# Second expert's routing list moved ahead of the first expert's products, with its 0/1 matrices on VectorE and Silu's table loaded earlier

## The chip, the cores and the metric

The kernel runs on one core of one Trainium2 chip. The metric is the device time of one execution in microseconds; of several executions the median is taken. The core has TensorE (PE, with its weight loads PEld), VectorE (DVE), ScalarE (ACT), GpSimd (POOL) and SyncE (SP), which work through a queue of instructions each, in order, and wait for one another by semaphores. SyncE and GpSimd issue the DMAs.

## What is computed

One layer of a hybrid encoder over 512 tokens of width 1024: a Mamba-2 mixer and a forget-gate attention side by side, an output projection, a LayerNorm, then a mixture of experts with a second LayerNorm. The change is in the mixture, of which the reference is:

```python
g_logits = (hf @ rg_w + rg_b)                       # 4 groups
g_val, g_idx = lax.top_k(jax.nn.softmax(g_logits), 1)
e_logits = ...                                      # the 4 experts of the chosen group
e_val, e_idx = lax.top_k(jax.nn.softmax(e_logits), TOP_K)   # 2 of them
weights = g_val[:, None] * e_val / sum(e_val)
for e in range(N_EXPERTS):                          # 16
    act = jax.nn.silu(hf @ w_gate[e]) * (hf @ w_up[e])
    out = out + combine[:, e:e + 1] * (act @ w_down[e])
```

Each expert has w_gate and w_up of 1024x512 and w_down of 512x1024, in float32.

## The kernel before

**Stages.** Projections, scan and attention come first; in the last part of the attention the output projection (L807) and the LayerNorm of four blocks of 128 tokens (hh[0] to hh[3]) run. From each block the router's logits are computed, `choose` ranks them and `seat` numbers the tokens of each expert in `place` (token rows by expert). Then 16 experts are worked through, e = 0 to 15, called the first, second, third expert and so on here.

**An expert.** At most 128 tokens are taken for it. Its list comes in four steps. `seats_of` (L937) compares the seat numbers 1 to 128 with `place`, one 128x128 compare for each of the four token blocks, and so makes four 0/1 matrices `se` in bf16. `list_of` multiplies them by `entry` on TensorE (L945) into a PSUM bank `plist`; `entry` holds the token number in two columns and the token's weight in three (each weight is split into three bf16 parts, L1324 and L1326). VectorE reduces the bank to the index `ix` (L950, L951) and the weight `wc` (L954). `gather` (L958) is an indirect DMA, issued by GpSimd, that fetches the 128 token rows from the stored `hb` into `xgs[e % 2]`. `call(e)` does these steps in turn; with `weights=False` only the token columns are multiplied, and the `se` are kept for the weights later.

**Products.** All products are in float32 by splitting: each operand has a high part, rounded by ScalarE (`eh` of the weights L987, `xgh` of the tokens L90), and a low part, the difference by VectorE (`el` L988, `xgl` L91); high x high, low x high and high x low are summed in PSUM. `gate_up(e)` (L1004 to L1006) goes through eight pieces of gate and up weights, in four steps of two pieces and 12 products; four buffers of `eh` and four of `el` go round. Then Silu on ScalarE (L1012) and the product with up on VectorE (`ac`, L1014 or L1016) follow. `xg_T` (L980) transposes the next expert's gathered rows on TensorE into `pxg`, `act_T` (L1022) transposes `ac` into `pat`, and `down` runs one expert later, inside the loop of the next. So between the first expert's last product and the second's first one there is no down product.

**The first expert** doesn't wait for all tokens. Its rows of the first two blocks are gathered ahead (`gather_first`), and those of the last two are picked from hh[2] and hh[3] with 0/1 matrices `pick` (L1296); both are summed on TensorE in the banks `px` (L1291), already transposed. Then `split` makes `xgh` and `xgl` of px.

**Weights.** `weigh()` is a generator: up to its `yield` it forms the exponentials (Exp on ScalarE, L1305 and L1314), after it the weights of both chosen experts (L1316 to L1326) into `entry`. The router calls its first half by `next(wg)`; the second half is emitted by `drop(wg)` after the first expert's early steps.

**What sets the order.** TensorE's order is that of the code (`MANUAL`). VectorE, ScalarE and GpSimd keep the code's order inside `with tc.manual_schedule(engines=VECTOR)` (the router, L1334 on); what comes after it, such as `call` in the expert loop and the second half of `weigh`, is placed by the scheduler, which may also put it among the router's own instructions. In the expert loop `gate_up(0)` is advanced by three steps (`EARLY`); the second expert's `call(1, False)` comes after the first of these steps, the third's `call(2, False)` after the third. `weights_of_first()`, in the second expert's turn, makes the first expert's list, then the weights of the second and third, then counts the tokens (`pcnt`, L1413). `bank("s", ...)` gives these lists two PSUM banks in turn.

Of the kernel before, what the change touches and what calls it, by code (L numbers as in the profile page):

```python
# [40 lines left out]
EARLY = 3  # L41
# [28 lines left out]
def hybrid_layer(ctx: ExitStack, tc: tile.TileContext, x, xT, wu, w16, bT, bz, bv, b16, cw, cb,  # L70
# [861 lines left out]
    def seats_of(pool, place_, eng):  # L932

        r = (Q("se") if pool is lp else pool.tile([P, 256], F32, name="se")).bitcast(BF16)
        r = [r[:, t * P:(t + 1) * P] for t in range(NT)]
        for t in range(NT):
            eng.tensor_scalar(r[t], seats, place_(t), None, op0=OP.is_equal)  # L937
        return r
# [26 lines left out]
    def entry_of(e):  # L965
        return lambda t: entry[:, t, EO[e]]

    def call(e, weights=True):
        se = seats_of(lp, lambda t: place[:, t, EO[e]:EO[e] + 1], G)
        ix, wc = list_of(lp, se, entry_of(e), weights=weights)  # L970
        gather(ix, xgs[e % 2])
        lists[e] = [ix, wc if weights else se]
# [325 lines left out]
    def weigh():  # L1298

        gs, r1, wv, mx, gx = R([], "gs"), R([], "r1"), R([2], "wv"), R([5], "mx"), R([4], "gx")  # L1300
        oh = [R([4, 4], "oh") for _ in range(2)]
        lr = rows_(lg4)
        V.tensor_reduce(rows_(mx), lr, axis=AX.X, op=OP.max)
        V.tensor_tensor(lr, lr, over(rows_(mx), 4), op=OP.subtract)
        A.activation(gx, lg4[:, :, 0], AF.Exp)  # L1305
        og = CH["og"][:, :, :, None].to_broadcast([P, NT, 4, 4])
        for k in (1, 0):
            V.scalar_tensor_tensor(oh[k], CH["rank"][:, :, 1:5], float(k), og, op0=OP.is_equal, op1=OP.mult)
            if k:
                t_ = R([4, 4], "t_")  # L1310
                V.tensor_tensor(t_, oh[k], lg4[:, :, 1:5], op=OP.mult)
                oh0, oh1 = (o_.rearrange("p t g e -> p t (g e)") for o_ in oh)
                V.tensor_reduce(r1, t_.rearrange("p t g e -> p t (g e)"), axis=AX.X, op=OP.add)
                A.activation(r1, r1, AF.Exp)  # L1314
        yield
        V.tensor_reduce(gs, gx, axis=AX.X, op=OP.add)  # L1316
        V.scalar_tensor_tensor(gs, r1, 1.0, gs, op0=OP.add, op1=OP.mult)
        V.reciprocal(wv[:, :, 0], gs)
        V.tensor_tensor(wv[:, :, 1], wv[:, :, 0], r1, op=OP.mult)
        for k, o_ in enumerate((oh0, oh1)):  # L1320
            V.scalar_tensor_tensor(o_, o_, 1.0 / ALPHA, over(wv[:, :, k], 16), op0=OP.mult, op1=OP.mult)
        V.tensor_tensor(oh0, oh0, oh1, op=OP.add)
        for j in range(2, 5):
            V.tensor_copy(entry[:, :, :, j], oh0)  # L1324
            if j < 4:
                V.tensor_tensor(oh0, oh0, entry[:, :, :, j], op=OP.subtract)  # L1326
# [7 lines left out]
    with tc.manual_schedule(engines=VECTOR):  # L1334
        for t in range(NT):
            ph_ = proj_half(t, 0)
            if t == 3:
                next(ph_)
                seat(0, 2)
                gf = gather_first()  # L1340
                next(gf)
                next(ph_)
                u_T(2, 0)
                u_T(2, 1)
                drop(gf)
                norm_gain(2)
            drop(ph_)
            if t in DSP0:
                dsp[0, DSP0.index(t)] = wsplit(raw[0, DSP0.index(t)])
            if t:  # L1350
                norm_shift(t - 1)
                if t < 3:
                    u_T(t - 1, 0)
                    u_T(t - 1, 1)
                    norm_gain(t - 1)
                norm_bias(t - 1)
            ph_ = proj_half(t, 1)
            if t < 3:
                if t == 2:
                    logits(1)  # L1360
                    norm_store(1, hb, G)
                    norm_store(1, ub, G)
                    choose(0, 2)
                drop(ph_)
                norm_stats(t)
                if t == 1:
                    logits(0)
                    norm_store(0, hb, G)
                    norm_store(0, ub, G)
        next(ph_)  # L1370
        next(ph_)
        u_T(3, 0)
        drop(ph_)
        logits(2, range(3))
        px_open()
        u_T(3, 1)
        logits(3, range(4))
        norm_stats(3)
        norm_store(2, hb, G)
        norm_shift(3)  # L1380
        norm_gain(3)
        logits(3, range(4, 8))
        px_open()
        logits(2, range(3, 8))
        choose(2, 4)
        px_add(xgs[0], identf, range(KC))
        seat(2, 4)
        for t in (2, 3):
            picks(t)
        norm_bias(3)  # L1390
        norm_store(3, hb, G)
        px_add(hh[2], pick[2], range(KC))
        dsp[0, 2] = wsplit(raw[0, 2])
        wg = weigh()
        next(wg)
        xt_ = [wide("x", n, NX).rearrange("p (k s) -> p k s", s=P) for n in ("xgh", "xgl")]
        for hf in range(2):
            px_add(hh[3], pick[3], range(4 * hf, 4 * hf + 4), True)
            split(*(t_[:, hf * 4:hf * 4 + 4] for t_ in xt_), px[hf].rearrange("p (k s) -> p k s", s=P))
        for t in range(2, 4):  # L1400
            norm_store(t, ub, G)
        load_pieces(NPRE, NPRE + GATED, G)
        dsp[0, 3] = wsplit(raw[0, 3])

    def weights_of_first():

        lists[0] = list_of(lp, seats_of(lp, lambda t: place[:, t, EO[0]:EO[0] + 1], G), entry_of(0))
        for e in (1, 2):
            lists[e][1] = list_of(lp, lists[e][1], entry_of(e), tokens=False)[1]

        pn = bank("s", "pcnt")[:, :16]
        for tt in range(NT):
            T.matmul(pn, lhsT=onesb, rhs=mskb[:, tt], start=(tt == 0), stop=(tt == NT - 1))  # L1413
        V.tensor_reduce(cnt_i, pn, axis=AX.X, op=OP.max)
        rt.close()

    at = {}
    for e in range(NEXP - 2):
        load_pieces(NPRE + 12 * e + (0 if e else GATED), NPRE + 12 + 12 * e)
        gu = gate_up(e, xt_, "pj" if e else "o")  # L1420
        for n in range(EARLY):
            next(gu)
            if e == 0 and n == 0:
                call(1, False)
        call(e + 2, bool(e))
        if e == 0:
            drop(wg)
        if e == 1:
            weights_of_first()
        drop(gu)  # L1430
        xt_ = xg_T(xgs[(e + 1) % 2])
        for d in DOWN[e]:
            def between(f):
                if f == ACT_AT and d != e and e in DOWN[e]:
                    at[e] = act_T(e)
            finish(d, down(d, at.pop(d), between=between))
        if e not in DOWN[e]:
            at[e] = act_T(e)
# [182 lines left out]
```

## Time and profile before

| what | us |
|---|---|
| median of 3 runs | 629.06 |
| lowest and highest of them | 626.08, 634.25 |
| the profiled execution | 632.85 |
| its span, first to last instruction | 631.1 |
| TensorE busy in the span | 578.6 (92%) |
| VectorE busy | 526.4 (83%) |
| ScalarE busy | 409.7 (65%) |
| GpSimd busy | 195.8 (31%) |

All durations are of the one profiled execution, in us from the span's start. Busy shares are means over stages with different limits: what a change is worth is read where it stands. A duration of a TensorE product includes its way through the array; the pitch from one start to the next is what it takes from the stream.

### The profile page before, as it was taken

What the parts mean: (1) busy time and instruction counts of PE and PEld (TensorE: products, weight loads), DVE (VectorE), ACT (ScalarE), POOL (GpSimd) and SP (SyncE); (2) the same over time, 40 slices, a digit from 0 to 9 for tenths busy, and PEclk for the clock granted to TensorE, in tenths of its full rate; (3) what the DMA queues carried; (4) which work ended last, traced back from release to release, by engine and by line L of the source; (5) the groups of instructions that cost most, each with busy time, mean ns of one, the idle gap of its engine ahead of it and who ended that gap; (6) DMA issues with size and microseconds to landing.
All of it is one profiled execution on the core that took longest, in us unless ns stands there. A gap on an engine that the chain in (4) does not pass through costs nothing.

```text
span 631.1 us, 9108 instructions
## 1 busy us (share of the span) xinstructions
PE 578.6 (92%) x3020; PEld 472.7 (75%) x3021; DVE 526.4 (83%) x904; ACT 409.7 (65%) x640; POOL 195.8 (31%) x221
## 2 busy tenths in 40 slices
PE   6997997899999989999789999999999999999790
PEld 4786887788777758778667888888888888877550
DVE  3897598888668787668778999999999999999883
ACT  5575363543577776422267888888888888888660
POOL 6300000033553441014472223433343233412341
PEclk9998898999999999999889999999999999999996
DMA  8621021221222174994799999999999999998531
GB/s 264 209 68 60 8 77 59 84 68 65 70 68 66 36 238 133 389 344 175 281 389 319 304 382 344 386 361 358 355 346 342 328 352 373 346 339 287 190 122 61
DMA packets 62102, 142.73 MB, mean 226 GB/s; under 512 B 10073, under 2 KB 10073, under 8 KB 62048
## 3 DMA queue, kind: packets, MB, share of 16 engines
q1 hardware_dynamic: 55712, 127.88, 56.4%
q0 software_dynamic: 6336, 14.20, 7.6%
q8 instruction: 25, 0.41, 0.3%
q14 instruction: 29, 0.24, 0.1%
HBM read 136.26 MB, written 14.68 MB: 239 GB/s over the span
## 4 chain that ended last, share of the span: by engine, by line
PE 52%; DVE 16%; DMA 16%; issue 7%; ACT 6%; POOL 2%; POOLq 0%; SPq 0%; ACTq 0%; DVEq 0%
DMA xg<-ub,ix 6%; PE pw L807 4%; PE pg L1004 4%; PE pg L1006 4%; PE pg L1005 4%; PE pjT L241 4%; PE pu L1004 4%; PE pu L1006 4%; PE pu L1005 4%; PE py L1043 3%; PE py L1041 3%; PE py L1042 3%; DMA ub<-yo,ix 3%; PE pjR L265 3%; DMA xg<-hb,ix 2%
## 5 line engine op out<-in xcount | busy, mean ns | idle before, releaser
L987 ACT ACTIVATE eh<-wf 128x1024 fp32r<-128x1024 f32 x188 | 198.7, 1060 | 49.6 <-PE pg L1006 16.4
L1004 PE MATMUL pg<-eh,xgh 128*128 128x512 f32 x128 | 53.3, 416 | 0.8 <-ACT xgh L90 0.8
L958 POOL DMA_INDIRECT xg<-hb,ix x16 | 21.5, 1343 | 99.9 <-PE pg L1006 77.6
L1006 PE MATMUL pg<-eh,xgl 128*128 128x512 f32 x128 | 50.2, 393 | 1.3 <-DVE xgl L91 1.3
L1049 POOL DMA_INDIRECT ub<-yo,ix x14 | 27.2, 1945 | 74.5 <-ACT at L90 57.7
L937 POOL TENSOR_SCALAR se<-seats,place 128x128 bf16<-128x128 f32 x64 | 49.5, 784 | 1.6 <-PE pat L1022 1.1
L1004 PE MATMUL pu<-eh,xgh 128*128 128x512 f32 x128 | 49.9, 390 | 0.0
L1006 PE MATMUL pu<-eh,xgl 128*128 128x512 f32 x128 | 49.8, 389 | 0.0
L1041 PE MATMUL py<-eh,at 128*128 128x512 f32 x120 | 48.5, 404 | 1.0 <-ACT at L90 0.7
L241 PE MATMUL pjT<-xh,wh 128*128 128x512 f32 x112 | 47.6, 425 | 1.6 <-DVE kl L671 1.6
L1043 PE MATMUL py<-eh,at 128*128 128x512 f32 x120 | 47.1, 392 | 0.0
L241 PE MATMUL pjT<-xh,wl 128*128 128x512 f32 x112 | 45.0, 402 | 0.0
L241 PE MATMUL pjT<-xl,wh 128*128 128x512 f32 x112 | 45.0, 402 | 0.0
L265 PE MATMUL pjR<-wh,xh 128*128 128x256 f32 x128 | 38.6, 302 | 1.2 <-DVE vf L643 1.2
L265 PE MATMUL pjR<-wl,xh 128*128 128x256 f32 x128 | 37.5, 293 | 0.0
L265 PE MATMUL pjR<-wh,xl 128*128 128x256 f32 x128 | 37.4, 292 | 0.0
L130 POOL TENSOR_TENSOR rst<-rst,mhalf 128x1 f32<-128x1 f32 x8 | 4.6, 578 | 100.5 <-DVE rst L129 100.5
L1006 PEld LDWEIGHTS pg<-eh,xgl 128*128 128x128 f32 x128 | 24.1, 188 | 7.4 <-DVE xgl L91 2.2
L225 POOL TENSOR_TENSOR wl<-wr,wh 128x512 fp32r<-128x512 f32 x16 | 21.4, 1362 | 25.9 <-ACT wh L220 25.9
L1004 PEld LDWEIGHTS pg<-eh,xgh 128*128 128x128 f32 x128 | 24.2, 189 | 5.3 <-ACT xgh L90 1.2
L220 ACT ACTIVATE wh<-wr 128x1024 fp32r<-128x1024 f32 x22 | 23.1, 1054 | 7.5 <-PE pjT L241 3.4
L1006 PEld LDWEIGHTS pu<-eh,xgl 128*128 128x128 f32 x128 | 24.0, 188 | 5.1
(971 smaller groups left out, 1756.4 us busy)
## 6 DMA issues: line engine op xcount, KB each, us to landing
wf<-in_w_up SPq DMA_DIRECT2D x64, 512.0 KB
wf<-in_w_gate SPq DMA_DIRECT2D x64, 512.0 KB
wf<-in_w_down SPq DMA_DIRECT2D x62, 512.0 KB
wr<-in_wu SPq DMA_DIRECT2D x22, 512.0 KB
wor<-in_w_out SPq DMA_DIRECT2D x8, 512.0 KB
hh<-in_x SPq DMA_DIRECT2D x4, 512.0 KB
hb<-hh POOLq DMA_DIRECT2D x4, 512.0 KB, 4.8
ub<-hh POOLq DMA_DIRECT2D x4, 512.0 KB, 5.6
```

The source lines that it names most:

```text
L220: A.activation(h_, wr_, AF.Copy)
L241: T.matmul(pt, lhsT=w_[:, k % 4, m * P:(m + 1) * P], rhs=x_[k], start=(i == 0), stop=(i == 23))
L265: T.matmul(pt, lhsT=x_[k][:, t * P:(t + 1) * P], rhs=w_[:, k % 4, :], start=(i == 0), stop=(i == 23))
L807: T.matmul(pw, lhsT=m_[k][:, ts_], rhs=wo[k][w_][:, c_], start=(i == 0), stop=(i == 11))
L937: eng.tensor_scalar(r[t], seats, place_(t), None, op0=OP.is_equal)
L987: A.activation(h_, src, AF.Copy)
L1004: T.matmul(pt, lhsT=h_[:, k], rhs=wh_[:, f], start=(k == 0), stop=False)
L1005: T.matmul(pt, lhsT=h_[:, k], rhs=wl_[:, f], start=False, stop=False)
L1006: T.matmul(pt, lhsT=l_[:, k], rhs=wh_[:, f], start=False, stop=(k == KC - 1))
L1041: T.matmul(pt, lhsT=h_[:, f], rhs=wh_[:, c_], start=(f == 0), stop=False)
L1043: T.matmul(pt, lhsT=l_[:, f], rhs=wh_[:, c_], start=False, stop=(f == 3 and rows is None))
L1049: G.indirect_dma_start(out=ub, out_offset=bass.IndirectOffsetOnAxis(ap=ix, axis=0), in_=yo, in_offset=None, bounds_check=S - 1, oob_is_err ...
```

## The change

- The second expert's 0/1 matrices are made by VectorE, in the router, right after the LayerNorm's last step (`se1`), and its list and gather are called in the router, before the first expert's products, instead of after the first of the early steps.
- The first expert's 0/1 matrices, for its weights, are made earlier, after the third expert's call; its list is multiplied after the weights of the second and third expert instead of before them.
- A Silu of a 128x4 tile that nobody reads follows the second Exp; the load of Silu's table comes there.

```diff
-    def call(e, weights=True):
-        se = seats_of(lp, lambda t: place[:, t, EO[e]:EO[e] + 1], G)
+    def call(e, weights=True, se=None):
+        se = se or seats_of(lp, lambda t: place[:, t, EO[e]:EO[e] + 1], G)
...
                 A.activation(r1, r1, AF.Exp)
+
+                A.activation(R([], "tab"), r1, AF.Silu)
         yield
...
         norm_store(3, hb, G)
+        se1 = seats_of(lp, lambda t: place[:, t, EO[1]:EO[1] + 1], V)
         px_add(hh[2], pick[2], range(KC))
...
             split(*(t_[:, hf * 4:hf * 4 + 4] for t_ in xt_), px[hf].rearrange("p (k s) -> p k s", s=P))
+        call(1, False, se1)
         for t in range(2, 4):
             norm_store(t, ub, G)
...
     def weights_of_first():
 
-        lists[0] = list_of(lp, seats_of(lp, lambda t: place[:, t, EO[0]:EO[0] + 1], G), entry_of(0))
         for e in (1, 2):
             lists[e][1] = list_of(lp, lists[e][1], entry_of(e), tokens=False)[1]
+        lists[0] = list_of(lp, lists[0], entry_of(0))
...
-        for n in range(EARLY):
+        for _ in range(EARLY):
             next(gu)
-            if e == 0 and n == 0:
-                call(1, False)
         call(e + 2, bool(e))
         if e == 0:
             drop(wg)
+            lists[0] = seats_of(lp, lambda t: place[:, t, EO[0]:EO[0] + 1], G)
```

What stands where, before (-) and now (+). First VectorE, between the LayerNorm's last step (L1182) and the router's weights (`arena` tiles hold their small operands):

```order
 L1182 SCALAR_TENSOR_TENSOR hh<-hh,rs_3307,l1b 128x1024
-L988 TENSOR_TENSOR el__3365<-wf,eh 128x1024
+L937 TENSOR_SCALAR se<-seats,place 128x128 x4
+L988 TENSOR_TENSOR el__3370<-wf,eh 128x1024
 L1303 TENSOR_REDUCE arena_3188<-lg_3028 128x20
```

Four compares are added ahead of a weight piece's low part. A little further on VectorE's queue comes to the low half of the first expert's tokens (L91, twice):

```order
+L1323 SCALAR_TENSOR_TENSOR arena_3373<-arena_3373,arena_3188 128x64
+L1324 TENSOR_TENSOR arena_3188<-arena_3188,arena_3373 128x64
+L1326 CAST entry<-arena_3188 128x64
+L1328 TENSOR_TENSOR arena_3188<-arena_3188,entry 128x64
+L1326 CAST entry<-arena_3188 128x64
+L1328 TENSOR_TENSOR arena_3188<-arena_3188,entry 128x64
+L1326 CAST entry<-arena_3188 128x64
 L91 TENSOR_TENSOR xgl<-px,xgh 128x512 x2
-L1321 SCALAR_TENSOR_TENSOR arena_3368<-arena_3368,arena_3188 128x64
-L988 TENSOR_TENSOR el__3398<-wf,eh 128x1024
-L1322 TENSOR_TENSOR arena_3188<-arena_3188,arena_3368 128x64
```

The seven operations that end the weights have moved from behind the low halves to in front of them. On ScalarE, at the same place, the high halves of the tokens (L90) follow the two Exp:

```order
 L1305 ACTIVATE arena_3188<-lg_3028 128x16
 L1314 ACTIVATE arena_3188<-arena_3188 128x4
+L1316 ACT_TABLE_LOAD
+L1316 ACTIVATE arena_3373<-arena_3188 128x4
 L90 ACTIVATE xgh<-px 128x512 x2
 L987 ACTIVATE eh<-wf 128x1024 x7
-L1012 ACT_TABLE_LOAD
```

The table's load has moved from the first Silu to in front of the high halves. On GpSimd, after the stores of the normalized blocks, xg_3013 is the buffer of the second expert's gather:

```order
 L1188 DMA hb<-hh 128x1024 x2
+L937 TENSOR_SCALAR se<-seats,place 128x128 x8
+L958 DMA xg_3013<-hb,ix 128x1024
 L1188 DMA ub<-hh 128x1024 x2
 L925 DMA wf<-in_w_down 128x1024 x2
-L937 TENSOR_SCALAR se<-seats,place 128x128 x8
-L958 DMA xg_3013<-hb,ix 128x1024
```

Eight compares stand in front of the gather as before, now those of the third and the first expert; four DMA issues have moved behind it. Last, VectorE at `weights_of_first`, as it stands now (the fourth expert's index and weight, the second's weight, a weight piece, the third's weight, the first's list, the count):

```order
L950 TENSOR_REDUCE if__3669<-plist 128x1
L954 TENSOR_REDUCE wc<-plist 128x1
L951 TENSOR_SCALAR ix<-if__3669 128x1
L954 TENSOR_REDUCE wc<-plist 128x1
L988 TENSOR_TENSOR el__3766<-wf,eh 128x1024
L954 TENSOR_REDUCE wc<-plist 128x1
L950 TENSOR_REDUCE if__3697<-plist 128x1
L954 TENSOR_REDUCE wc<-plist 128x1
L951 TENSOR_SCALAR ix<-if__3697 128x1
L1418 TENSOR_REDUCE cnt_i<-pcnt 128x1
```

Before, the first expert's three reductions stood ahead of the second's weight, and the weight piece between the second's and the third's:

```order
L950 TENSOR_REDUCE if__3682<-plist 128x1
L954 TENSOR_REDUCE wc<-plist 128x1
L951 TENSOR_SCALAR ix<-if__3682 128x1
L954 TENSOR_REDUCE wc<-plist 128x1
L988 TENSOR_TENSOR el__3765<-wf,eh 128x1024
L954 TENSOR_REDUCE wc<-plist 128x1
L1414 TENSOR_REDUCE cnt_i<-pcnt 128x1
```

The weight piece keeps its place behind the second expert's weight; what has moved is that the first expert's reductions come behind both.

## Rows read from the trace of the kernel before

**Rows 1.** Windows: busy us by engine, PEclk, DMA share, GB/s.
```profile
303.00:304.00 1.00, 0.71 (x3) 0.71 (x4) 0.31 (x2) 0.00 (x0) 0.00 (x0) 0.50 0.90 295
...
327.00:328.00 1.00, 0.89 (x4) 0.89 (x5) 0.00 (x0) 0.00 (x0) 1.00 (x3) 0.50 1.02 377
350.00:360.00 10.00, 10.00 (x49) 8.09 (x48) 10.00 (x13) 7.88 (x10) 1.85 (x1) 1.00 0.93 294
```

**Rows 2.** Timeline of TensorE: start, us, engine, line, operation, [idle before <- releaser].
```profile
303.29 3.50 PE L1291 MATMUL px<-identf,xg 128*128 128x128 f32 x16 [1.71 <-DMA xg<-hb,ix]
...
307.62 3.84 PE L1291 MATMUL px<-xg,hh 128*128 128x128 f32 x32 [0.67 <-DVE xg L1296]
...
313.11 0.50 PE L1006 MATMUL pg<-eh,xgl 128*128 128x512 f32 x1 [0.37 <-DVE xgl L91]
...
323.87 0.39 PE L1006 MATMUL pu<-eh,xgl 128*128 128x512 f32 x1
327.11 1.97 PE L980 MATMUL pxg<-identf,xg 128*128 128x128 f32 x8 [2.85 <-DMA xg<-hb,ix]
...
330.44 0.40 PE L1006 MATMUL pg<-eh,xgl 128*128 128x512 f32 x1
```

**Rows 3.** Timeline of GpSimd, 309 to 332 us.
```profile
309.32 0.53 POOL L1188 DMA_DIRECT2D hb<-hh  x1 [9.12 <-DVE hh L1182]
...
311.99 7.27 POOL L937 TENSOR_SCALAR se<-seats,place 128x128 bf16<-128x128 f32 x8
319.72 1.39 POOL L958 DMA_INDIRECT xg<-hb,ix  x1 [0.46 <-issue]
...
329.60 2.34 POOL L937 TENSOR_SCALAR se<-seats,place 128x128 bf16<-128x128 f32 x4 [1.09 <-PE pat L1022]
```

**Rows 4.** VectorE's groups by form, 290 to 343 us: busy, mean ns | idle before.
```profile
L1324 DVE CAST entry<-arena 128x64 bf16<-128x64 f32 x3 | 0.8, 263 | 0.0
...
L1273 DVE TENSOR_SCALAR se<-seats,place 128x128 bf16<-128x128 f32 x2 | 0.5, 282 | 0.0
...
L1326 DVE TENSOR_TENSOR arena<-arena,entry 128x64 f32<-128x64 f32 x2 | 0.4, 224 | 0.0
...
L1322 DVE TENSOR_TENSOR arena<-arena,arena 128x64 f32<-128x64 f32 x1 | 0.4, 385 | 0.0
...
L1321 DVE SCALAR_TENSOR_TENSOR arena<-arena,arena 128x64 f32<-128x64 f32 x1 | 0.2, 207 | 0.0
```

**Rows 5.** Timeline of VectorE, 312 to 327 us.
```profile
312.38 1.27 DVE L91 TENSOR_TENSOR xgl<-px,xgh 128x512 fp32r<-128x512 f32 x2
...
326.28 0.41 DVE L1016 TENSOR_TENSOR ac<-sg,pu 128x256 f32<-128x256 f32 x1
```

**Rows 6.** Timeline of ScalarE, 311 to 330 us.
```profile
311.27 0.21 ACT L1314 ACTIVATE arena<-arena 128x4 f32<-128x4 f32 x1 [0.43 <-DVE arena L1313]
311.38 1.07 ACT L90 ACTIVATE xgh<-px 128x512 fp32r<-128x512 f32 x2
...
322.44 1.28 ACT L1012 ACT_TABLE_LOAD   x1
323.74 0.38 ACT L1012 ACTIVATE sg<-pg 128x256 f32<-128x256 f32 x1
...
329.61 1.05 ACT L987 ACTIVATE eh<-wf 128x1024 fp32r<-128x1024 f32 x1
```

**Rows 7.** Timeline of TensorE and VectorE at the lists, 338 to 341 us.
```profile
338.10 1.23 DVE L988 TENSOR_TENSOR el__3755<-wf,eh 128x1024 fp32r<-128x1024 f32 x1
...
339.51 0.51 PE L945 MATMUL plist<-entry,se 128*128 128x3 bf16 x8 [0.99 <-DVE wc L954]
...
339.80 0.16 DVE L954 TENSOR_REDUCE wc<-plist 128x1 f32<-128x3 f32 x1
...
339.88 1.23 DVE L988 TENSOR_TENSOR el__3765<-wf,eh 128x1024 fp32r<-128x1024 f32 x1
...
340.02 0.24 PE L1413 MATMUL pcnt<-mskb,onesb 128*128 128x16 bf16 x4
```

## Prediction

> **What bounds the kernel now.** I read the windows first, then TensorE's timeline, then that of each engine it waits for. From 350 us on TensorE is busy in all of a 10 us window, at granted clock 1.00 [rows 1]; it goes on so, expert after expert, to the last ones. A delay or a gain before that point is therefore carried to the end one for one. So the question is when that dense stretch begins, and the change works just ahead of it, between 307 and 341 us. There the reader is to see three things. First, TensorE finishes gathering the first expert's tokens (the px products, 32 from 307.62 for 3.84, so until 311.46) and its first product with the low half of the tokens starts at 313.11 [rows 2]. Second, the last product of the first expert starts at 323.87 and, with the products at a pitch of about 0.23, ends near 324.1; then TensorE waits 2.85 for the second expert's gather, and the first transposes after it, 8 in 1.97, run at granted clock 0.50 [rows 1, 2]. Third, at 339.51 a 0.99 wait for VectorE stands inside the lists [rows 7].
>
> The gather that it waits for started at 319.72, behind eight 0/1 compares on GpSimd from 311.99 to 319.26, and behind four more DMA issues from 309.85 on, where the store of 309.32 ends [rows 3]. From its start to the transposes of 327.11 are 7.39.
>
> **The change part by part.** Times are those of the profiled execution (632.85 us, span 631.1), and the sum is a difference against it; it lies 3.8 above the median 629.06 of the runs, whose own spread is 626.08 to 634.25. I carry the difference over to the median.
>
> (1) The gather comes earlier, by less than the words of the change say. VectorE makes the second expert's compares, but the order shows that GpSimd still has eight in front of the gather, now those of the third and the first expert. Only the four DMA issues go behind it. So the compares start at 309.85 instead of 311.99 and, at the same 7.27, end at 317.1; with the 0.46 that lay between compares and gather the gather starts near 317.6, its list being ready at 316.7 (low halves of (2) from 315.0 for 1.27, two reductions of 0.15 and their handovers), and its rows are there 7.39 later, at 325.0. At the 0.59 a compare that four took from 329.60 [rows 3], instead of 0.91, the list would be what it waits for: 324.2. The stores and loads moved behind it are not needed before the second expert is through.
>
> (2) The first products start later, because of VectorE. Before, the low half (xgl, L91) starts at 312.38 [rows 5]. Now four compares stand ahead of it; two took 0.5, 0.282 each [rows 4], so four are 1.13 by durations, about 0.9 end to end. And the rest of the weights (seven small operations: one L1321 of 0.21, L1322 0.39, three L1324 of 0.263, two L1326 of 0.224, together 1.83 [rows 4]), which before ran after the low half, stand ahead of it as well, as the order shows. By durations 2.96; eleven short operations overlap by up to 0.07 each, 2.2 at least. I take 2.6: the low half starts at 315.0, the first product with it at 315.7 for 313.11.
>
> (3) ScalarE's table. The load took 1.28 at 322.44, and Silu's first use followed at 323.74 [rows 6]; there it delayed nobody, for TensorE waited for the gather until 327.11. It now stands between the Exp of 311.27 and the copies xgh of 311.38, which TensorE's first products read. Exp ends about 311.5 + 0.9 (the compares) = 312.4; load 1.28 and the small Silu 0.21 (as the Exp row) make 313.9, the first copy (half of 1.07) 314.4. So the high half comes 2.4 late, but the low half of (2) is later still, and the load costs nothing of its own; without (2) it would be the bound. The Trainium skill ("ScalarE: Activation LUTs", What ACT_TABLE_LOAD costs) counts a drain of about 1.38 us beside the load, about 2.66 in all. By that rule the high half would be there at 315.8, TensorE at 316.4 and the sum 0.7 larger; here Silu starts 1.30 after the load does, so the trace shows no such drain.
>
> (4) The clock. Between the px products with the new list (until about 311.6) and the first product at 314.4 TensorE has nothing to do for 2.8. After gaps of 1.71 and 2.85 the rows show clock 0.50, the 1.2 GHz level (windows 303 and 327); after 0.67 the products of 307.62 ran at 0.12 each, near the pace of 2.4 GHz [rows 1, 2]. 16 products took 3.50 at the low clock, 32 took 3.84 at the full one [rows 2], so such a stretch loses up to 3.50 - 1.92 = 1.6. A part of it falls on the wait for the low half; I take 1.0, bounds 0 and 1.6.
>
> (5) End of the first expert: 324.1 + 2.6 - 0.1 (a list moved out of it) + 1.0 = 327.6. The gather is there at 325.0, so that wait is gone, but the transposes start 0.5 later than at 327.11. What is late next is ScalarE and VectorE: the order puts the copy and the difference of the second expert's fourth weight piece in front of the tokens' split, and the copy waits for the last product to release its buffer. Copy 1.05 [rows 6], difference 1.23 [rows 7], product ac 0.41, low half 0.64 [rows 5], and four handovers: about 3.4 from the transposes' start to the first low product. Before, with the transposes at half clock, it was 330.44 - 327.11 = 3.33 [rows 2]. So the half clock that goes is replaced by a chain as long: +0.1, together +0.6.
>
> (6) In that chain TensorE works about 1.8 of 3.4, with two waits of roughly 1 us. Whether the clock falls then no row shows; bounds 0 and 1.6. I take 0.9, for the two waits add up to about the gap of 1.71, whose row is the nearest.
>
> (7) The lists' new order. Two PSUM banks serve four lists and the count in turn: before the fourth expert's, the first's, the second's weights, the third's weights; now fourth, second, third, first. So before, the count at 340.02 needed a bank that the second expert's reduction at 339.80 set free, ahead of the 1.23 difference of 339.88 [rows 7]. Now it needs the third expert's reduction, which the order has behind that difference: 339.6 + 1.23 + 0.15 = 341.0. The 0.99 wait stays. +1.0, bounds 0.6 (VectorE comes early to the difference by the 0.4 that ScalarE's copy leaves it) and 1.4 (difference and reduction in full). Two waits near 1 us so close together may lower the clock again: 0 to 1.6, I take 0.3, for the 0.99 alone did not.
>
> Sum: 0.6 + 0.9 + 1.0 + 0.3 = +2.8: 629.1 + 2.8 = 631.9 (635.65 on the profiled execution's own scale). Nothing later in the kernel moves: instruction orders are the same from the third expert on.
>
> **Rivals.** *The table holds the tokens* (3): if ScalarE needs as long again as the 1.28 of the load before its next use, the high half ends at 312.4 + 2.56 + 0.21 + 0.53 = 315.7 and the low half 0.64 after it, 0.6 to 0.7 later than in (2): 632.6. For it speaks only that before the load of the row no Exp stood; against it the 1.30 of the row. The drain of the Trainium skill's page named above would be such a cost.
>
> *The clock falls fully at all three gaps* (4, 6, 7): 1.6 + 1.6 + 1.6 for 1.0 + 0.9 + 0.3, so 2.6 more: 634.5. For it speaks that both long gaps of the trace were followed by 0.50; against it that busy pieces lie in the second and third.
>
> *The gather's gain is kept* (other side, not slower): TensorE keeps its full clock at 311 to 316 and after, and the small operations run at their closest, 2.2. Then the first expert ends at 324.1 + 2.2 - 0.1 = 326.2, the transposes start 0.9 earlier than before, the chain adds 0.1, the lists 0.6: -0.2 or, with the lists' wait hidden too, -0.8. Time 628.3 to 628.9, say 628.5. It decides at the transposes: before 326.6 this case holds, after it mine. For it: the stall of 2.85 and the half clock after it are in the chain of waits and do go. Against it: a 2.8 gap that no row shows without a fall.
>
> **How the numbers follow.** My sum 0.5, the table 0.1, the clock at all gaps 0.2, the gain kept 0.2. Predicted 631.9. The terms' bounds give 628.3 to 634.5; medians of a few runs of a kernel whose runs spread over 8 us can lie 2 to 3 further out on both sides: 626.5 to 637.5, beyond which I leave 2 in 10 at most. Only 2%, 12.6 us, can be told from no change in a measurement of this kernel; no case comes near it. Faster by over 2% 0.01, within 0.97, slower 0.02 for a mechanism that I have not seen, such as a clock that stays low.
>
> **What would show it.** Right: gather issued near 317.6 and no wait for it; the first low product near 315.7 with VectorE's weights right before it; clock 0.50 within 312 to 319; transposes near 327.6; the count's product waiting for VectorE about 1 us after the second wait of the lists. Wrong: a full clock through 319 and transposes before 326.6 (gain kept); VectorE waiting for ScalarE's xgh ahead of the low half (the table); a gather that still ends last there, if compares on GpSimd take longer than 0.91 each.

## The result and the profile after

| | before | changed |
|---|---|---|
| median of 19 runs each, us | 629.05 | 631.51 |
| lowest and highest | 622.07, 634.25 | 628.97, 637.73 |
| ratio to before, 95% interval | | 1.0062 [1.0037, 1.0087] |
| the profiled execution, and its span | 632.85, 631.1 | 629.41, 627.7 |

The forecast was 631.9. The change costs 0.6%, clear of zero.

The profiled execution of the changed kernel is one of its faster ones, that of before one of its slower, and the ratio leaves out runs over 1.5% above a kernel's fastest while the medians take all. Its 32 px products start 4.16 earlier, at 303.46 for 307.62 [rows 2], in stretches that the change does not touch: the granted clock of before reads 0.91, 0.83 and 0.91 in 0:20, 60:80 and 100:120, that of the changed kernel 1.00, 0.93 and 1.00. So both traces are read from that start on, called the px start below. First TensorE's timeline of the changed kernel:

```profile
start us, us, engine line op out<-in xcount [idle before <-releaser]
...
303.46 6.17 PE L1291 MATMUL px<-xg,hh 128*128 128x128 f32 x32 [0.67 <-DVE xg L1296]
309.46 0.24 PE L945 MATMUL plist<-entry,se 128*128 128x2 bf16 x4
310.25 0.50 PE L1004 MATMUL pg<-eh,xgh 128*128 128x512 f32 x1 [0.54 <-ACT xgh L90]
...
311.48 0.50 PE L1006 MATMUL pg<-eh,xgl 128*128 128x512 f32 x1 [0.49 <-DVE xgl L91]
...
322.03 0.40 PE L1006 MATMUL pu<-eh,xgl 128*128 128x512 f32 x1
322.26 1.04 PE L980 MATMUL pxg<-identf,xg 128*128 128x128 f32 x8
324.07 0.44 PE L1022 MATMUL pat<-identf,ac 128*128 128x128 f32 x2 [0.77 <-DVE ac L1016]
325.54 0.44 PE L1022 MATMUL pat<-identf,ac 128*128 128x128 f32 x2 [1.03 <-DVE ac L1016]
...
326.28 0.39 PE L1006 MATMUL pg<-eh,xgl 128*128 128x512 f32 x1
...
335.37 0.42 PE L945 MATMUL plist<-entry,se 128*128 128x3 bf16 x8 [1.00 <-DVE wc L954]
336.75 0.24 PE L1417 MATMUL pcnt<-mskb,onesb 128*128 128x16 bf16 x4 [0.96 <-DVE wc L954]
...
340.49 0.48 PE L1041 MATMUL py<-eh,at 128*128 128x512 f32 x1
```

Against [rows 2], the first product with the tokens' low half (called the first low product) comes 8.02 after the px start, not 5.49. The 2.85 wait for the gather is gone: behind the first expert's last product (322.03) the transposes follow at once, and two waits, 0.77 and 1.03, for `ac` stand there instead. The lists have a second wait, 0.96, beside the 0.99 of [rows 7]. From the px start to the first py product it is 37.03; before, with that product at 343.76, it was 36.14. The rest of the span is as long as before, 287.2 for 287.3.

What the first products wait for stands on VectorE:

```profile
304.78 0.87 DVE L937 TENSOR_SCALAR se<-seats,place 128x128 bf16<-128x128 f32 x4
...
310.63 0.26 DVE L1326 CAST entry<-arena 128x64 bf16<-128x64 f32 x1
310.74 1.28 DVE L91 TENSOR_TENSOR xgl<-px,xgh 128x512 fp32r<-128x512 f32 x2
...
312.12 0.15 DVE L951 TENSOR_SCALAR ix<-if__3403 128x1 int32<-128x1 f32 x1
```

and on ScalarE:

```profile
307.99 0.20 ACT L1314 ACTIVATE arena<-arena 128x4 f32<-128x4 f32 x1 [0.53 <-DVE arena L1313]
308.21 1.28 ACT L1316 ACT_TABLE_LOAD   x1
309.51 0.21 ACT L1316 ACTIVATE arena<-arena 128x4 f32<-128x4 f32 x1
309.62 1.07 ACT L90 ACTIVATE xgh<-px 128x512 fp32r<-128x512 f32 x2
```

The low half starts right behind the last small operation of the weights (310.63), and the copies, behind table and Silu, end at 310.69: two delays side by side. GpSimd shows the gather:

```profile
305.80 5.52 POOL L937 TENSOR_SCALAR se<-seats,place 128x128 bf16<-128x128 f32 x8
313.04 1.37 POOL L958 DMA_INDIRECT xg<-hb,ix  x1 [1.72 <-PE pg L1006]
314.42 1.11 POOL L1188 DMA_DIRECT2D ub<-hh  x2
315.52 1.05 POOL L925 DMA_DIRECT2D wf<-in_w_down  x2
```

It is issued 9.58 after the px start, before 12.10 [rows 3]. The eight compares end at 311.32 and no longer hold it. Its index `ix` is ready at 312.27, behind the low halves, and 0.77 passes until the gather starts; the profile puts the end of this wait down to a product with the low half (L1006). Either stands behind the low halves. The clock, in windows (a stretch and its length, five engines' busy time, granted clock, DMA share, GB/s):

```profile
303.00:304.00 1.00, 0.54 (x2) 0.54 (x3) 0.96 (x4) 0.00 (x0) 0.00 (x0) 0.50 0.00 0
308.00:309.00 1.00, 1.00 (x9) 1.00 (x9) 0.93 (x6) 0.98 (x2) 1.00 (x3) 0.82 0.93 238
312.00:319.00 7.00, 7.00 (x32) 5.77 (x32) 6.17 (x8) 5.09 (x5) 3.52 (x5) 1.00 0.64 212
```

Here it read 0.50 (1.2 GHz) before 308, so the px products took 6.17 for 3.84 and filled most of the gap ahead of the first product. Behind it the clock held, where the forecast had it at 0.50.

### The profile page after: what moved, and what is told of

Read it like the earlier page. It is cut to its first block, busy times and chain, and to the rows that moved or that the text cites. A ratio compares the mean times of both kernels' runs of the same rounds, so it can differ in the third digit from the quotient of the medians.

```text
span 627.7 us, 9112 instructions
## 1 busy us (share of the span) xinstructions
PE 576.2 (92%) x3021; PEld 470.4 (75%) x3021; DVE 527.2 (84%) x908; ACT 410.0 (65%) x641; POOL 192.1 (31%) x217
## 4 chain that ended last, share of the span: by engine, by line
PE 53%; DVE 17%; DMA 14%; issue 7%; ACT 6%; SPq 1%; POOL 1%; POOLq 0%; ACTq 0%; DVEq 0%
DMA xg<-ub,ix 6%; PE pg L1004 4%; PE pg L1006 4%; PE pw L807 4%; PE pg L1005 4%; PE pu L1004 4%; PE pu L1006 4%; PE pu L1005 4%; PE pjT L241 4%; PE py L1043 4%; PE py L1041 4%; PE py L1042 3%; DMA ub<-yo,ix 3%; PE pjR L265 3%; DVE acc L433 2%
## 5 line engine op out<-in xcount | busy, mean ns | idle before, releaser
L1006 PE MATMUL pg<-eh,xgl 128*128 128x512 f32 x128 | 50.2, 393 | 1.4 <-DVE xgl L91 1.4
L1006 PE MATMUL pu<-eh,xgl 128*128 128x512 f32 x128 | 49.9, 389 | 0.0
L937 POOL TENSOR_SCALAR se<-seats,place 128x128 bf16<-128x128 f32 x60 | 44.5, 751 | 1.9 <-PE pat L1022 1.4
L265 PE MATMUL pjR<-wh,xh 128*128 128x256 f32 x128 | 37.1, 290 | 1.2 <-DVE vf L643 1.2
L265 PE MATMUL pjR<-wl,xh 128*128 128x256 f32 x128 | 36.1, 282 | 0.0
L265 PE MATMUL pjR<-wh,xl 128*128 128x256 f32 x128 | 36.0, 281 | 0.0
L1006 PEld LDWEIGHTS pg<-eh,xgl 128*128 128x128 f32 x128 | 24.0, 188 | 7.5 <-DVE xgl L91 2.3
L1006 PEld LDWEIGHTS pu<-eh,xgl 128*128 128x128 f32 x128 | 24.0, 188 | 5.1
```

Of the source, the lines that this page charges most:

```text
L265: T.matmul(pt, lhsT=x_[k][:, t * P:(t + 1) * P], rhs=w_[:, k % 4, :], start=(i == 0), stop=(i == 23))
L1006: T.matmul(pt, lhsT=l_[:, k], rhs=wh_[:, f], start=False, stop=(k == KC - 1))
```

## Experiments

D1 is the distance from the px start to the first low product, D2 from the first expert's last product to the second expert's first low product, D from the px start to the first py product. The changed kernel's first trace has 8.02, 4.25 and 37.03, that of before 5.49, 6.57 and 36.14. "Mean clock" is the granted clock, as the mean over a kernel's runs. The kernel before was run beside each group of kernels.

**The changed kernel again**, without an edit.

> The changed kernel once more, for a second trace. Three distances tell the theories apart, from the px products with the last block (x32) on: D1, from their start to the first product with a low half (before 5.49, changed 8.02); D2, from the start of the first expert's last product to the second expert's first product with a low half (before 6.57, changed 4.25); the waits inside the lists (before 0.99, changed 0.99 and 0.96); D, from the px products' start to the first py product (before 36.14, changed 37.03). Theory (the instructions cost +0.9, the rest of the measured difference is TensorE's clock, which falls at the new gaps in some executions and not in others): D1 7.8 to 8.3 where the clock is full ahead of it, D2 4.2 at full clock and up to 1.6 more where the granted clock reads 0.50, lists 2.0; D 37.0 with no fall, 38 to 39 with one; median 630 to 633. Rival (the order alone decides): D 37.0 whatever the clock reads, and the median within 1.0 of the kernel before plus 0.9.

Measured: 631.31, ratio 1.0057 [1.0021, 1.0094]; D1 8.01, D2 4.25, lists as forecast, but D 40.22. On its TensorE the px products ran at full clock and left a gap of 2.88:

```profile
302.69 3.84 PE L1291 MATMUL px<-xg,hh 128*128 128x128 f32 x32 [0.67 <-DVE xg L1296]
309.48 0.50 PE L1004 MATMUL pg<-eh,xgh 128*128 128x512 f32 x1 [2.88 <-ACT xgh L90]
```

Its windows behind that gap and behind the lists:

```profile
311.00:315.00 4.00, 4.00 (x12) 3.08 (x11) 2.84 (x5) 1.46 (x2) 2.72 (x4) 0.58 0.24 82
339.00:343.00 4.00, 4.00 (x17) 3.25 (x16) 1.68 (x2) 2.21 (x3) 1.84 (x4) 0.58 1.05 383
```

Same order, same waits; the clock fell behind both. From the first low product to the first expert's last one it took 12.17 for 10.55, behind the lists 1.58 more: the 3.2 by which D differs is clock alone. Over 31 runs the changed kernel's mean clock is 0.9749, over 101 of before 0.9802. By that the changed kernel spends some 6.7 us more of a run at 1.2 GHz.

**The weights' second half behind the split**: the call moves from the expert loop to the end of the router.

```diff
         dsp[0, 3] = wsplit(raw[0, 3])
+        drop(wg)
...
-            drop(wg)
```

> The changed kernel with the second half of the weights' operations behind the tokens' split. Theory (two bounds in a row: VectorE's small operations first, ScalarE's table load right behind): D1 falls from 8.0 only to 7.5, VectorE then waiting for xgh; D2, where the order now has the weight piece's difference behind the tokens' low half, falls from 4.25 to 3.4; time 1.4 less than the changed kernel, 630.1. Rival A (the small operations alone decide): D1 5.8 to 6.0, time 3 less. Rival B (the table load keeps ScalarE longer than its 1.28, and decides already): D1 8.0 as before, time 0.9 less.

Measured: 631.34, ratio 1.0060 [1.0022, 1.0099]. The first product still comes 6.79 after the px start, and now VectorE waits for ScalarE too:

```profile
310.77 1.29 DVE L91 TENSOR_TENSOR xgl<-px,xgh 128x512 fp32r<-128x512 f32 x2 [1.95 <-ACT xgh L90]
310.79 0.79 PE L1004 MATMUL pg<-eh,xgh 128*128 128x512 f32 x1 [2.87 <-ACT xgh L90]
```

The low half starts 6.77 after the px start, for 7.28, so the small operations alone were worth 0.5. D1 is 7.81, with the products ahead of it at half clock (0.79 and 0.63 for 0.50 and 0.40). With the small operations gone the table holds the products almost as long. D2 stayed at 4.28, a miss. There is no gain in time.

**The old order of the lists.**

```diff
+        lists[0] = list_of(lp, lists[0], entry_of(0))
         for e in (1, 2):
             lists[e][1] = list_of(lp, lists[e][1], entry_of(e), tokens=False)[1]
-        lists[0] = list_of(lp, lists[0], entry_of(0))
```

> The changed kernel with the first expert's list again ahead of the weights of the second and third. Theory (a bank freed behind a weight piece's difference costs 0.96 in the new order): one wait of about 1.0 in the lists instead of two, the count's product right behind the lists, D 36.1 for 37.0, time 0.9 to 1.0 less, 630.5. Rival (the new order has only moved a wait which the next products would have had anyway): the first product after the lists waits instead, D 37.0, time the same.

Measured: 630.38, ratio 1.0031 [0.9999, 1.0064]. There is one wait of 1.00, the lists are over in 1.85 for 2.73, and the products behind them don't come later: the 0.9 is real in the trace. The time doesn't show it: the interval overlaps with the changed kernel's, 1.0021 to 1.0094. D was 38.57, for behind the first gap the clock read 0.50 from 312 to 318, and the first expert's products took 13.02 for 10.55.

**No early Silu.**

```diff
-                A.activation(R([], "tab"), r1, AF.Silu)
```

> The changed kernel without the early Silu, so that its table is loaded again at the first expert's own Silu. Theory (early, the load is hidden behind VectorE; late, it is no longer hidden, for the gather's wait is gone): D1 7.9 to 8.0, unchanged though xgh comes 1.5 earlier; D2 5.5 for 4.25, since the copies behind the Silu come 1.28 later; time 1.2 more than the changed kernel, 632.7. Rival A (the early load is what makes the first products late): D1 6.5 to 7.0, D2 5.5, time the same. Rival B (the late load stands beside other work): D2 4.25, time the same or less.

Measured: 628.91, ratio 1.0008 [0.9962, 1.0053], beside the changed kernel's 1.0057; the intervals overlap. The theory fell by its distances: D1 is 6.13 and D2 3.58. At D1 rival A was nearest, at D2 rival B. VectorE without the Silu:

```profile
309.85 0.22 DVE L1323 SCALAR_TENSOR_TENSOR arena<-arena 128x64 f32<-128x64 f32 x1
309.98 1.28 DVE L91 TENSOR_TENSOR xgl<-px,xgh 128x512 fp32r<-128x512 f32 x2
...
311.25 0.21 DVE L1323 SCALAR_TENSOR_TENSOR arena<-arena,arena 128x64 f32<-128x64 f32 x1
```

and ScalarE:

```profile
309.12 0.20 ACT L1314 ACTIVATE arena<-arena 128x4 f32<-128x4 f32 x1 [0.54 <-DVE arena L1313]
309.23 1.07 ACT L90 ACTIVATE xgh<-px 128x512 fp32r<-128x512 f32 x2
...
321.46 1.28 ACT L1012 ACT_TABLE_LOAD   x1
322.76 0.38 ACT L1012 ACTIVATE sg<-pg 128x256 f32<-128x256 f32 x1
```

Seven of VectorE's operations on the weights, from the second L1323 on, now stand behind the tokens' split, though no line on them was touched. With the Silu the split has to wait for ScalarE, and the operations stand in that hole. That the scheduler puts them there because of the hole is a guess; the two orders are shown. The late load costs nothing in the trace: Silu starts before the first expert's last product, and the chain behind it is shorter, since the order now puts the tokens' low half ahead of the fourth weight piece.

**The early Silu alone, in the kernel before.**

```diff
                 A.activation(r1, r1, AF.Exp)
+                A.activation(R([], "tab"), r1, AF.Silu)
```

> The kernel before with the early Silu alone. In its order all small operations of the weights now stand ahead of the tokens' split on VectorE, though nothing else was moved. Theory (the early table is the root of the late first products: it holds the tokens' copies, and the scheduler fills VectorE's wait with the weights): D1 7.1 for 5.49; the first expert ends 1.6 later, but the gather still ends last there (wait 1.2 to 1.4 for 2.85), so D2 5.0 and D 36.1 as in the kernel before; time within 1 of it. Rival (the compares on VectorE and the early list are the root, the table is harmless): D1 5.5, D2 6.6, D 36.1. The two differ in D1 alone.

Measured: 631.66, ratio 1.0103 [1.0068, 1.0139]. That is more than the whole change's 1.0057 and 1.0062, though the intervals overlap. D1 is 7.41, near the theory's 7.1, but D 38.21. TensorE waits 2.06 for the copies,

```profile
303.21 3.84 PE L1291 MATMUL px<-xg,hh 128*128 128x128 f32 x32 [0.67 <-DVE xg L1296]
309.11 0.79 PE L1004 MATMUL pg<-eh,xgh 128*128 128x512 f32 x1 [2.06 <-ACT xgh L90]
```

the window behind that reads half clock,

```profile
309.00:316.00 7.00, 6.59 (x18) 4.49 (x19) 4.57 (x8) 3.25 (x5) 4.49 (x6) 0.51 1.02 372
```

and GpSimd has its compares done long before the gather:

```profile
307.58 5.91 POOL L937 TENSOR_SCALAR se<-seats,place 128x128 bf16<-128x128 f32 x8
318.63 1.94 POOL L958 DMA_INDIRECT xg<-hb,ix  x1 [5.14 <-PE pu L1006]
```

Two things were missed. The first expert's products took 13.23 for 10.76, by the clock. And in the kernel before the gather's list stands behind the first of these products, so that late products make a late gather: issued 15.4 after the px start, not 12.1. The wait that was to hide the delay moved along with it.

**Fillers in the changed kernel's gaps**: products on constants, which nobody reads. 8 stand ahead of the first product (behind `call(1, False, se1)`), 3 ahead of the first and of the third pat transpose, 3 behind each of two lists.

```diff
+    def fill_(n):
+        fb = bank("t", "idle")
+        for _ in range(n):
+            T.matmul(fb, lhsT=identb, rhs=identb[:, None, :].to_broadcast([P, 4, P]), start=True, stop=True)
```

> The changed kernel with products on constants that nobody reads in the gaps which the change leaves on TensorE: 8 of 128x512 before the first expert's first product, 3 and 3 in the two waits ahead of the second expert, 3 and 3 between the lists. Theory (the clock falls at these gaps in most executions and costs 1 to 3 us): from the first low product to the first expert's last one 10.55, from the count to py 3.74, D 37.0 in the trace, mean granted clock of the runs 0.978 or more for 0.975, time 1.5 less than the changed kernel, 629.9. Rival (the clock falls whatever TensorE does there, or the fillers get in the way): D above 38, time the same or 0.5 more.

Measured: 632.89, ratio 1.0120 [1.0070, 1.0170]. The first expert took 10.56 at full clock, but D2 was 7.98. The bank of the fillers is one of those that the tokens' transposes use, and TensorE waited until these were read:

```profile
323.14 1.04 PE L980 MATMUL pxg<-identf,xg 128*128 128x128 f32 x8
327.02 1.35 PE L1273 MATMUL idle<-identb 128*128 128x512 bf16 x3 [2.84 <-DVE xgl L91]
```

**Fillers in the first gap alone**: `fill_(8)` in the changed kernel, `fill_(6)` behind the split in the kernel before with the early Silu.

```diff
         call(1, False, se1)
+        fill_(8)
```

> The changed kernel with 8 fillers in one gap alone, ahead of the first expert's first product, where the trace of the changed kernel shows 2.9 of idle TensorE at full clock. Theory (the clock that falls behind this gap is the largest part of the change's cost; 1.6 in the second trace): from the first low product to the first expert's last one 10.55, D1 8.0, D2 4.25; mean clock of the runs 0.978 to 0.980 for 0.975, time 1.5 less than the changed kernel. Rival (the fall only moves to the next gap): 10.55 too, but half clock later in the trace, mean clock 0.975, time the same.

> The kernel before with the early Silu and 6 fillers ahead of the first expert's first product. The early Silu alone made that kernel 1.0% slower (0.7 to 1.4), though by its trace the first expert's later end is hidden by the gather's wait: D was 38.2, of which 2.5 stood in the first expert's products at granted clock 0.50. Theory (the loss is the clock that falls in the 2.1 of idle TensorE ahead of the first product): from the first low product to the first expert's last one 10.8 (13.2 without fillers), D 35.7, mean clock 0.978 or more for 0.974, ratio 1.002 to 1.005. Rival (the loss is not the clock; the weights' small operations or the table's hold cost it elsewhere): 10.8 too, but ratio 1.008 or more.

Measured: 631.10, ratio 1.0037 [1.0002, 1.0072], mean clock 0.9788; and 630.57, ratio 1.0023 [0.9988, 1.0058], mean clock 0.9793. The first expert's products took 10.55 and 10.77, as forecast. In the second pair the intervals with and without fillers (1.0103) lie apart, which speaks for the clock behind the first gap. How much of the loss was clock stays open: D is no shorter with fillers, the medians of the two kernels are 1.1 apart, and the kernel before had 625.17 beside the one and 629.29 beside the other. In the first pair the intervals overlap. Both traces show a fall at the next waits, ahead of the second expert; here the changed kernel's:

```profile
325.00:329.00 4.00, 4.00 (x12) 3.13 (x11) 2.15 (x3) 1.33 (x2) 1.06 (x2) 0.57 1.04 390
```

D was 38.65 and 38.30, not the 37.0 of the changed kernel's first trace and the 35.7 forecast (in the second a wait of 2.28 for the gather adds to it). Filling one gap raised the mean clock and did not spare each execution its fall.

**No early Silu, and all lists in one bank**: the products of the lists and of the count first, the reductions behind them. The second kernel adds fillers, `fill_(6)`, `fill_(2)`, `fill_(5)` and `fill_(5)` ahead of the two px groups, the first product and the pat transposes.

```diff
-        for e in (1, 2):
-            lists[e][1] = list_of(lp, lists[e][1], entry_of(e), tokens=False)[1]
-        lists[0] = list_of(lp, lists[0], entry_of(0))
-
-        pn = bank("s", "pcnt")[:, :16]
+        pb = bank("s", "plist")
+        for e, se in ((1, lists[1][1]), (2, lists[2][1]), (0, lists[0])):
...
+        pn = pb[:, 32:48]
```

> The changed kernel without the early Silu, and with all products of the lists and of the count written into one bank first and reduced afterwards. Theory (with the table's hold and the bank's wait gone the early gather's gain is left): D1 6.1, D2 3.6, no wait in the lists, D 32.5 at full clock and about 34 with one fall; time 2.0 less than the variant without the early Silu alone and 1.0 to 2.0 less than the kernel before, near 626. Rival (the products after the lists wait for their wc instead): lists short, but count to py 1 longer, D 34.5 or more, time as without the early Silu alone.

> The last variant with fillers in TensorE's gaps: 6 and 2 ahead of the two px groups, 5 ahead of the first product, 5 ahead of the second expert. Theory: granted clock 1.00 from 297 us on in the trace, D 32.5, runs' mean clock 0.982 or more, time 1 to 1.5 less than without fillers, near 624.5. Rival (fillers hold real products back or the clock falls anyway): D 33.5 to 34.5, time the same.

Measured: 629.47, ratio 1.0040 [1.0003, 1.0077], and 626.08, ratio 1.0026 [0.9992, 1.0061]. In both D1 is 6.13 and the lists take 0.41 without a wait. With fillers D is 33.98, of which 2.17 are again a filler's wait, and so 2.2 less than before; the time did not follow. ScalarE shows why, at the load of `u` for the closing LayerNorm. Before, it waits 0.49 for it:

```profile
590.02 1.06 ACT L1079 ACTIVATE junk<-u 128x1024 f32<-128x1024 f32 x1 [0.49 <-DMA u<-ub]
```

With one bank and fillers it waits 3.06:

```profile
585.02 1.06 ACT L1081 ACTIVATE junk<-u 128x1024 f32<-128x1024 f32 x1 [3.06 <-DMA u<-ub]
```

The last weight load was issued 232.3 after the first py product; before and in the changed kernel it was 227.3 and 227.6. The stream of weights used to follow TensorE and now held the end. The windows of 15 us from the px start say where it fell behind. Before:

```profile
307.62:322.62 15.00, 14.08 (x82) 11.51 (x83) 14.64 (x33) 8.89 (x12) 11.29 (x14) 1.00 0.82 302
```

The changed kernel:

```profile
303.46:318.46 15.00, 13.96 (x69) 12.22 (x70) 13.83 (x34) 8.38 (x12) 9.64 (x14) 0.84 0.47 157
```

That is 302 GB/s and 157: 2.2 MB less by then, or 6 us at the 365 GB/s of 360 to 440 us. The kernel with one bank and fillers has 199.

**Stores and loads ahead of the gather again**, in the kernel without the early Silu and with one bank; first without fillers, then with `fill_(6)`, `fill_(2)`, `fill_(5)` and, in the bank of the pat transposes itself, `fill_(4)`.

```diff
-        call(1, False, se1)
         for t in range(2, 4):
             norm_store(t, ub, G)
         load_pieces(NPRE, NPRE + GATED, G)
+        call(1, False, se1)
```

> The variant without the early Silu and with one bank for the lists, now with the stores and the two weight loads issued by GpSimd again ahead of the second expert's gather, as in the kernel before. In the last variants the distance D shrank by 2 to 3 and the time did not, and ScalarE waited 3.1 to 4.8 for the load of u near the end. Theory (the issues moved behind the gather restart the weights' stream later, by some 3 us of bytes, and once TensorE is faster the stream's end decides): the first 8 weight loads of SyncE come within 15 us of the px start instead of 20, the last one at most 258.5 us after it (261.1, 260.5), the wait for u under 1.5; D as in the variant before, 32.2 at full clock; time 2 less, 1 to 2 under the kernel before. Rival (the stream is bound by its bytes from the start or by its buffers, the late restart is caught up): last load 260 to 261, wait for u 3 or more, time unchanged.

> The same with fillers in TensorE's gaps: 6, 2 and 5 ahead of the px groups and of the first product, and 4 ahead of the second expert, these now in the bank which the transposes behind them fill, so that they wait for nothing. Theory: clock 1.00 from 297 to 345 us, D2 3.6 (not 5.4 to 8.0 as with the fillers in the tokens' banks), D 32.2, mean clock 0.984, time 1 to 1.5 less than without fillers. Rival (the stream of weights holds the end): D 32.2 and a wait for u of 2 or more, time the same.

Measured: **623.73, ratio 0.9927 [0.9892, 0.9963]**, so faster than the kernel before by 0.7%; the interval also lies below that of the changed kernel. With fillers it is 625.32, ratio 0.9960 [0.9928, 0.9992]. The kernel without fillers differs from the first one of the last group in the place of that call alone, and their intervals lie apart. The window of 15 us, without fillers:

```profile
299.03:314.03 15.00, 13.20 (x78) 11.01 (x79) 14.46 (x35) 8.62 (x11) 10.00 (x11) 1.00 0.89 322
```

Its GpSimd:

```profile
301.26 1.06 POOL L1188 DMA_DIRECT2D ub<-hh  x2
302.31 1.06 POOL L925 DMA_DIRECT2D wf<-in_w_down  x2
306.62 1.31 POOL L958 DMA_INDIRECT xg<-hb,ix  x1 [3.25 <-PE pg L1006]
307.98 9.27 POOL L937 TENSOR_SCALAR se<-seats,place 128x128 bf16<-128x128 f32 x8
```

And its ScalarE at `u`:

```profile
577.35 1.06 ACT L1079 ACTIVATE junk<-u 128x1024 f32<-128x1024 f32 x1 [0.34 <-DMA u<-ub]
```

The gather loses nothing, for GpSimd waits 3.25 ahead of it all the same, and the order now has it ahead of the compares. The weights come at 322 GB/s, their last load 227.1 after the first py product; the wait for `u` is 0.34, D is 32.20 (D1 6.03, D2 3.19). The fillers added nothing: D was 32.21 with them, in the trace without them (a run of 619.43) the clock read 1.00 throughout this stretch as it was, the mean clock was 0.9807 with them and 0.9825 without, and the intervals overlap.

## Why the prediction was right, step by step

The time and the direction held: +2.8 forecast; +2.5 by the medians, +3.9 by the ratio (2.3 to 5.5). Times below are on the scale of before, 4.16 added to the changed trace; "317.20 for 317.6" is measured for forecast.

- (1) The gather was issued at 317.20 for 317.6, and nobody waited for it. Of the two things that I had ahead of it, the compares took 0.69 each and ended first, 1.72 ahead of it; what held it was the list, as I had it, or a product with the low half, as the profile has it.
- (2) First low product 315.64 for 315.7: the size was right.
- (3) "The load costs nothing of its own" is the step that failed. The copies were late by what I worked out (their first product at 314.41 for 314.4), and the load is hidden beside (2). But (2) is its doing for the larger part: without the Silu, D1 falls to 6.13, and with the Silu alone the kernel before loses 1.0%. I had taken the order as given and priced its parts one by one, where one part had made the others move. What VectorE's compares and the rest bring is the 0.64 between 5.49 and 6.13. The rival that the table holds the tokens for as long again fell with its price: Silu starts 1.30 after the load begins, in [rows 6], in the changed kernel and without the early Silu. The Trainium skill ("ScalarE: Activation LUTs", What ACT_TABLE_LOAD costs) counts a drain of about 1.38 us beside the load; none of these loads shows it.
- (4) For the clock behind the first gap I took 1.0. It was 0 in the first trace, where the clock was low ahead of the gap, and 1.62, 0.97 and 2.47 in the three others with the same gap of 2.9. The term was too small as a mean.
- (5) The transposes came at 326.42 for 327.6, or 326.6 without the 1.0 of (4). The chain from them to the second expert's first low product took 4.02 for 3.4: TensorE's order has the transposes of `ac` ahead of the second expert's products, and they waited. The term was too small by 0.6.
- (6) A fall of 1.6 came behind that chain's waits in two of the five traces that have them (1.6 by D of the changed kernel with fillers in the first gap, 38.65 for 37.03); I took 0.9 for each.
- (7) The lists took 0.87 more for 1.0, and the old order undoes it. A fall came behind them in one trace of five; I took 0.3.

Taken as means over these traces, the falls of (4), (6) and (7) come to some 1.3, 0.6 and 0.3, near the 2.2 forecast; without the clock the forecast is +0.6, and the first trace shows +0.9. So the total came out by sizes that are near and by misses that cancel.

By itself the first trace meets what I had named as a sign of being wrong: full clock from 313.2 through 319 and the transposes before 326.6. The rival in which the gather's gain is kept describes it in that, but not in its price: D is +0.9, not -0.2 to -0.8, for the chain behind the transposes is 0.7 longer than before, not 0.1. The rival of a fall at all gaps is nearer to the second: two falls, +4.1. The median lies between them. Fitted over the runs of all kernels, a microsecond more at 1.2 GHz goes with 0.35 of time, so the 6.7 of the changed kernel make 2.4 of the 4.4 by which its mean is longer. The other 2.0 is more than the 0.9 of the traces. Part of it may be noise, for the mean of the kernel before went from 625.5 to 628.7 between the groups, and the trace of before has a fall of its own in its chain; how much each is stays open.

That the stores and loads moved behind the gather "are not needed before the second expert is through" was right for this change, but it used up the lead of the weights. That showed only where TensorE became faster, and putting them back turned the shorter D into time.

## What to carry to other kernels

An operation moved early because its engine seems free can make a scheduler reorder another engine: build the kernel with that one line alone, and read the orders of the engines that wait for it. A delay with two causes side by side stays when one is removed; look for the one that the other follows from. When a shorter stretch doesn't shorten the time, look at the far end for a stream that used to follow TensorE and now leads it.

## What the hardware showed that was not expected

How often the clock falls weighs as much as the order does. With the px products at full clock, 2.06 to 2.88 of idle TensorE ahead of the first product was followed by granted clock 0.50 in all four traces that have it. 1.35 and 1.36 (no early Silu, and no early Silu with one bank, both without fillers) were followed by it as well; 1.26 (the best kernel) was not, nor was any wait of 1.13 or less at this place. But a wait's length alone doesn't settle it. The same 1.35 ahead of the second expert was followed by no fall in either of those two traces, and pairs of shorter waits, 0.77 with 1.03 and 0.99 with 0.96, were followed by one in some traces and not in others. A fall costs about 1.6 where TensorE is dense, and 2.5 in the two traces in which 0.50 stayed about twice as long. The two runs of the kernel before at the highest mean clock, 0.990, took 622.3 and 622.8, that at the lowest, 0.966, 631.8.
